# An FFN's up products: the side work as a pipeline of one step per product, sums of the weights ahead of their splits

## The chip, the cores and the metric

One core of a Trainium2 chip runs the whole kernel. The metric is device time in microseconds from the first to the last instruction, the median of several runs. In the profile PE is the engine for matrix products (its weight loads are listed apart as PEld), ACT, DVE and POOL are the engines for elementwise work (ScalarE, VectorE, GpSimd), and SP issues the transfers (DMAs). Each engine takes its own instructions strictly in order; an instruction that must wait holds up all that stand behind it on that engine.

## The reference

One block of a model with three mixers (a gated delta rule, an mLSTM and an S5 scan, with a projection before and one behind them), then the feed-forward part that matters here, for 2048 tokens, width 1024 and hidden width 2816, all in float32:

```python
def conv_ffn(x, w_up, conv_w, conv_b, w_down):
    h = causal_depthwise_conv(x @ w_up, conv_w) + conv_b      # 3 taps per channel
    gate, up = jnp.split(h, 2, axis=-1)
    return (jax.nn.silu(gate) * up) @ w_down
...
        x = x + y @ w_out[l]
        x = x + conv_ffn(rms_norm(x, norm2_w[l]), w_up[l], ffn_conv_w[l], ffn_conv_b[l], w_down[l])
    return rms_norm(x, final_norm_w)
```

## The kernel before, in words

**Stages.** The mixers and `out_proj` take about the first half of the span, then comes the feed-forward part: two halves of 1024 tokens, each with an up phase and a down phase. In an up phase `up_pair(hf, i)` is run for 22 pairs; pair i holds 128 gate columns and the 128 up columns that belong to them. After the 22 pairs the down phase multiplies two blocks of 512 tokens with `w_down`.

**Products.** The up product of a pair is a 2 x 2 block product (columns gate and up; tokens in two blocks of 512; the inner dimension of 1024 in two halves) done with 7 block products instead of 8. Each operand is split into a hi and a lo part of the matmul's type, and hi x hi, hi x lo and lo x hi are summed: 3 matmuls for each of 4 inner tiles, so 12 matmuls for a product and 84 for a pair. In the profile they are `psf<-bh,f_ph`, `psf<-bl,f_ph` and `psf<-bh,f_pl`; down products are called psd.

**Operands.** The token operands (`bh` from ACT, `bl` from DVE) are made once for each half, from the normed tokens in `h2_d`, by `build` (in a first version also by `first_build` while `out_proj` still runs, and by `rest_build` at the start of the first up phase). The weight operands are made anew for each pair. SP loads the two raw tiles `f_wr` of a pair (512 KB each, 4 buffers, so two pairs). POOL makes sums: S1 = a21 + a22, S2 = S1 - a11 (tiles `f_S`), a21 := a11 - a21 in place (`f_wr<-f_wr`), and S2' = a12 - S2. `split_part` makes a part out of a block: ACT copies it to the hi tile `f_ph`, POOL subtracts that from the block to give `f_pl`. The 7 parts of a pair are, in this order, of a11, S2, S1, a21, a22, a12, S2'. A ring holds 8 parts; `make()` makes one part each time it is called, once behind each product, and so part k of the next pair behind product k of this one.

**Behind a product.** `up_pair` takes what the 7 products give out of PSUM: `s1` is copied by ACT (`f_s`), DVE adds others to it (`f_u`, `f_w`), and from product 3 on the raw tiles of the result come (`f_rw`, DVE reading PSUM): r22 and r21 (up columns), r11 and r12 (gate columns). `conv` makes the 3 taps of a raw tile: ACT scales it with a bias into `f_cv` and copies two columns of halo in and out (`f_rw<-f_halo`, `f_halo<-f_rw`); DVE adds the two other taps (SCALAR_TENSOR_TENSOR, below also "taps"). `mid` lets ACT do silu on a gate tile, DVE multiply it by its up tile, and SP store it to `mid_d`, which the down phase reads.

**Order.** The order in the code of `up_pair` is the order in each engine's queue; other generators (operands, end of the layer before) are fitted in between by a planner, `drive`, by estimated times. In the kernel before, `conv` and `mid` run where they are called, each waiting for the one before, and `make()` runs after the work of its product.

## Time and profile before

| | |
|---|---|
| median of 3 runs | 3215.14 us (3211.07 to 3228.27) |
| profiled execution | 3215.11 us, span 3213.3 us |
| busy over the span | PE 87%, DVE 58%, ACT 41%, POOL 42% |
| first and last matmul of the first up phase | 1555.4 and about 2105 us |
| the second up phase | 2377 to 2932 us |
| granted PE clock, mean | 0.94 |

The profiled execution stands at the median. All engines' lines read "line engine operation out<-in", with the shapes, the count and the times; nearly all instructions carry the line of one helper, so the tile names tell what they are. Where a matmul's row ends in a bracket, it holds the idle time of PE before it and what ended it.

### The profile page before, as it was taken

How to read it: one execution, taken by the hardware profiler on the slowest of the kernel's cores; microseconds unless marked ns; L12 is line 12 of the kernel's file. 1: busy time of each engine (PE TensorE's matmuls, PEld its weight loads, DVE VectorE, ACT ScalarE, POOL GpSimd, SP SyncE). 2: the span in 40 equal slices, each digit the busy share in tenths (PEclk: the TensorE clock that was granted, in tenths of full speed). 3: DMA queues.
4: the chain of work that ended last, by engine and by line, in shares of the span. 5: the costliest groups of instructions: out<-in, count | busy, mean ns of one | idle time of the engine just before them, and what ended most of it. 6: DMA issues, size and time to landing. Idle time of an engine off the chain costs nothing. (4 is left out here: it accounts for less than half of the span.)

```text
span 3213.3 us, 39006 instructions
## 1 busy us (share of the span) xinstructions
PE 2804.3 (87%) x13298; PEld 2261.1 (70%) x13298; DVE 1862.8 (58%) x4296; ACT 1305.6 (41%) x2818; POOL 1342.9 (42%) x1046
## 2 busy tenths in 40 slices
PE   7796888979988897998888888889989888888997
PEld 5675777868877785877666666668767666666876
DVE  6874677687657866536455555573335555554143
ACT  4534354445443545224334433453223333344232
POOL 3350222223222422111455556545545555655553
PEclk9897899989999998999899999999989999998999
DMA  4222212232213333266322222154531222223443
GB/s 120 83 76 84 73 56 72 74 92 84 62 55 90 89 108 118 76 219 195 115 65 59 62 64 72 60 177 167 171 115 59 59 63 68 67 59 126 162 156 113
DMA packets 366540, 312.17 MB, mean 97 GB/s; under 512 B 41283, under 2 KB 303558, under 8 KB 366342
## 3 DMA queue, kind: packets, MB, share of 16 engines
q1 hardware_dynamic: 366342, 309.69, 31.3%
q8 instruction: 105, 1.72, 0.2%
q14 instruction: 93, 0.76, 0.1%
HBM read 244.48 MB, written 65.14 MB: 96 GB/s over the span
## 5 line engine op out<-in xcount | busy, mean ns | idle before, releaser
L169 POOL TENSOR_TENSOR f_pl<-f_wr,f_ph 128x512 fp32r<-128x512 f32 x360 | 520.6, 1462 | 576.3 <-ACT f_ph L169 576.3
L169 PE MATMUL psf<-bh,f_ph 128*128 128x512 f32 x1232 | 515.9, 419 | 93.6 <-ACT f_ph L169 85.3
L169 DVE SCALAR_TENSOR_TENSOR f_cv<-f_rw,fpar,f_cv 128x512 f32<-128x512 f32 x352 | 344.3, 989 | 399.7 <-ACT f_rw L169 393.4
L169 PE MATMUL psf<-bh,f_pl 128*128 128x512 f32 x1232 | 520.1, 422 | 50.0 <-POOL f_pl L169 49.3
L169 PE MATMUL psf<-bl,f_ph 128*128 128x512 f32 x1232 | 507.0, 411 | 0.6 <-DVE bl L169 0.6
L169 POOL TENSOR_TENSOR wl<-wr,wh 128x1024 fp32r<-128x1024 f32 x108 | 258.2, 2393 | 582.0 <-ACT wh L169 511.9
L169 PEld LDWEIGHTS psf<-bh,f_ph 128*128 128x128 f32 x1232 | 244.3, 198 | 177.3 <-ACT f_ph L169 116.7
L169 ACT ACTIVATE f_ph<-f_wr 128x512 fp32r<-128x512 f32 x360 | 216.7, 621 | 369.5 <-issue 179.5
L169 PEld LDWEIGHTS psf<-bh,f_pl 128*128 128x128 f32 x1232 | 244.2, 198 | 152.8 <-POOL f_pl L169 97.2
L169 PEld LDWEIGHTS psf<-bl,f_ph 128*128 128x128 f32 x1232 | 244.5, 198 | 58.1 <-DVE bl L169 1.1
L169 PE MATMUL psd<-f_ph,d_l 128*128 128x512 f32 x640 | 253.4, 396 | 18.2 <-DVE d_l L169 18.1
L169 PE MATMUL psd<-f_ph,d_h 128*128 128x512 f32 x640 | 252.5, 395 | 4.8 <-ACT d_h L169 4.8
L169 PE MATMUL psd<-f_pl,d_h 128*128 128x512 f32 x640 | 252.1, 394 | 0.1
L169 POOL TENSOR_TENSOR f_pl<-f_S,f_ph 128x512 fp32r<-128x512 f32 x132 | 169.0, 1294 | 143.2 <-ACT f_ph L169 138.0
L169 DVE TENSOR_TENSOR d_l<-d_x,d_h 128x512 fp32r<-128x512 f32 x80 | 69.5, 875 | 269.5 <-ACT d_h L169 260.9
L169 ACT ACTIVATE f_cv<-f_rw,fpar 128x512 f32<-128x512 f32 x176 | 142.4, 809 | 180.9 <-DVE f_rw L169 180.9
L169 ACT ACTIVATE f_ph<-f_S 128x512 fp32r<-128x512 f32 x132 | 77.8, 621 | 204.9 <-POOL f_S L169 204.9
L169 PEld LDWEIGHTS psd<-f_ph,d_l 128*128 128x128 f32 x640 | 121.9, 190 | 47.9 <-DVE d_l L169 22.7
L169 PEld LDWEIGHTS psd<-f_ph,d_h 128*128 128x128 f32 x640 | 122.2, 191 | 30.8 <-ACT d_h L169 5.6
L169 PEld LDWEIGHTS psd<-f_pl,d_h 128*128 128x128 f32 x640 | 122.1, 191 | 26.4 <-POOL f_pl L169 0.7
L169 ACT ACTIVATE wh<-wr 128x1024 fp32r<-128x1024 f32 x108 | 114.1, 1056 | 39.6 <-PE psz L169 17.9
L169 ACT ACT_TABLE_LOAD x83 | 106.5, 1283 | 32.2 <-DVE acc L169 29.5
(514 smaller groups left out, 6144.2 us busy)
## 6 DMA issues: line engine op xcount, KB each, us to landing
wr<-in_w_in_dram SPq DMA_DIRECT2D x104, 512.0 KB
f_wr<-in_w_up_dram SPq DMA_DIRECT2D x88, 512.0 KB
f_wr<-in_w_down_dram SPq DMA_DIRECT2D x88, 512.0 KB
mid_d<-f_cv SPq DMA_DIRECT2D x88, 256.0 KB
d_x<-mid_d SPq DMA_DIRECT2D x80, 256.0 KB
xt<-in_x_dram SPq DMA_DIRECT2D x16, 512.0 KB
y<-y_d SPq DMA_DIRECT2D x16, 512.0 KB
h_d<-n_h SPq DMA_DIRECT2D x32, 256.0 KB
```

Of the source, the lines that this page charges most:

```text
L169: return f(*args, **kw)
```

## The change

`up_pair` keeps a list, `self.later`, of work put off by a number of steps. Behind each product `due()` first runs what is due, then `make()`, and only then comes the product's own evacuation. `conv` is cut in two: ACT's share one step later, DVE's two taps two steps later; `mid` puts silu three steps behind its call and the product with its store four. The list is emptied behind the last pair of a half. In `make`, S1 and S2 of a pair are computed right behind part 6 of the pair before (`sum12`), a21 in step 1 and S2' in step 4, each two steps ahead of its split. Raw tiles that come free are loaded again when the next `make()` goes through (`freed`). In `build`, the hi copies of a group are issued together, then the lo parts, then the sums, with places between them where the planner may put other work.

```diff
@@ -1574,9 +1574,11 @@
     def operands(self, pool, n):
         return [[pool.tile([P, 4, BT], F32R, name=f"b{e}{o}") for e in "hl"] for o in range(n)]
 
-    def put(self, o, j, x, cols=slice(0, BT)):
+    def put_hi(self, o, j, x, cols=slice(0, BT)):
+        self.A.activation(out=self.bq[o][0][:, j, cols], in_=x, func=AF.Copy)
+
+    def put_lo(self, o, j, x, cols=slice(0, BT)):
         hi, lo = [t[:, j, cols] for t in self.bq[o]]
-        self.A.activation(out=hi, in_=x, func=AF.Copy)
         self.V.tensor_tensor(out=lo, in0=x, in1=f32(hi), op=ALU.subtract)
 
     def h_part(self, x, hf, j, kh, n, cols=slice(0, BT)):
@@ -1591,17 +1593,24 @@
             for c0 in range(0, BT, W):
                 cols = slice(c0, c0 + W)
                 b11, b12, b21, b22 = [self.h_part(tile(), hf, j, kh, n, cols) for kh in range(2) for n in range(2)]
-                yield b12, b22
-                self.put(0, j, b11, cols)
-                if len(self.bq) > 5:
-                    self.put(5, j, b21, cols)
-                    self.put(6, j, b22, cols)
+                first = [(0, b11)] + ([(5, b21), (6, b22)] if len(self.bq) > 5 else [])
+                yield b11, b12, b21, b22
+                for o, x in first:
+                    self.put_hi(o, j, x, cols)
+                yield self.bq[first[-1][0]][0][:, j, cols], 1.0
+                for o, x in first:
+                    self.put_lo(o, j, x, cols)
                 V.tensor_tensor(out=b22, in0=b22, in1=b12, op=ALU.subtract)
                 V.tensor_tensor(out=b12, in0=b12, in1=b11, op=ALU.subtract)
                 V.tensor_tensor(out=b11, in0=b22, in1=b11, op=ALU.add)
                 V.tensor_tensor(out=b21, in0=b21, in1=b11, op=ALU.subtract)
-                for o, x in ((3, b22), (2, b12), (1, b11), (4, b21)):
-                    self.put(o, j, x, cols)
+                yield b21, 2.0
+                then = ((3, b22), (2, b12), (1, b11), (4, b21))
+                for o, x in then:
+                    self.put_hi(o, j, x, cols)
+                yield self.bq[4][0][:, j, cols], 1.0
+                for o, x in then:
+                    self.put_lo(o, j, x, cols)
         self.built = True
 
     def first_build(self):
@@ -1613,7 +1622,8 @@
             for j in range(4):
                 x = self.h_part(tile(), 0, j, 1, n)
                 yield x
-                self.put(5 + n, j, x)
+                self.put_hi(5 + n, j, x)
+                self.put_lo(5 + n, j, x)
         self.rest = True
 
     def ffn_plan(self):
@@ -1629,6 +1639,7 @@
                 self.loads += [("M", hf * HALF + q * BT)] + [("D", m) for m in range(MF)]
         self.raws, self.parts, self.ring = [], [], NPART
         self.built = False
+        self.freed, self.sums, self.later = 0, None, []
         for _ in range(NRAW):
             self.raw_load()
 
@@ -1660,38 +1671,41 @@
         kind, j = self.todo[0]
         if kind == "U" and self.fu is None:
             return
+
+        while self.freed:
+            self.freed -= 1
+            self.raw_load()
         self.todo.pop(0)
         if kind != "U":
             w = self.raws.pop(0)
             for c in range(2):
                 self.split_part(w[:, 4 * c:4 * c + 4, :])
-            self.raw_load()
+            self.freed += 1
             return
         gate, up = self.raws[0:2]
         a11, a12, a21, a22 = gate[:, 0:4, :], gate[:, 4:8, :], up[:, 0:4, :], up[:, 4:8, :]
-        if j == 0:
-            self.split_part(a11)
-        elif j == 1:
-            self.s1, self.s2 = [self.fu.tile([P, 4, P], F32, tag="f_" + nm, bufs=2, name="f_" + nm)
-                                for nm in ("S1", "S2")]
-            G.tensor_tensor(out=self.s1, in0=a21, in1=a22, op=ALU.add)
-            G.tensor_tensor(out=self.s2, in0=self.s1, in1=a11, op=ALU.subtract)
-            self.split_part(self.s2)
-        elif j == 2:
-            self.split_part(self.s1)
-        elif j == 3:
+
+        if j == 0 and self.sums is None:
+            self.sum12()
+        if j == 1:
             G.tensor_tensor(out=a21, in0=a11, in1=a21, op=ALU.subtract)
-            self.split_part(a21)
         elif j == 4:
-            self.split_part(a22)
-        elif j == 5:
-            self.split_part(a12)
-        else:
-            G.tensor_tensor(out=self.s2, in0=a12, in1=self.s2, op=ALU.subtract)
-            self.split_part(self.s2)
+            G.tensor_tensor(out=self.sums[1], in0=a12, in1=self.sums[1], op=ALU.subtract)
+        s1, s2 = self.sums
+        self.split_part((a11, s2, s1, a21, a22, a12, s2)[j])
+        if j == 6:
             self.raws = self.raws[2:]
-            for _ in range(2):
-                self.raw_load()
+            self.freed += 2
+            self.sums = None
+            if self.todo and self.todo[0][0] == "U":
+                self.sum12()
+
+    def sum12(self):
+
+        gate, up = self.raws[0:2]
+        s1, s2 = self.sums = [self.fu.tile([P, 4, P], F32, tag="f_" + nm, bufs=2, name="f_" + nm) for nm in ("S1", "S2")]
+        self.G.tensor_tensor(out=s1, in0=up[:, 0:4, :], in1=up[:, 4:8, :], op=ALU.add)
+        self.G.tensor_tensor(out=s2, in0=s1, in1=gate[:, 0:4, :], op=ALU.subtract)
 
     def bank(self):
         tag = min(self.bufs, key=lambda n: self.clock.slot(n, self.bufs[n]))
@@ -1713,23 +1727,42 @@
             self.ring += 1
             return ps
 
+        def due():
+            now, self.later = [f for d, f in self.later if d == 0], [(d - 1, f) for d, f in self.later if d]
+            for f in now:
+                f()
+            self.make()
+
         def conv(rw, ci):
+
             halo = self.halo2[:, ci, :]
-            cv = tile("cv", 5)
-            A.activation(out=cv, in_=rw[:, 2:BT + 2], func=AF.Identity,
-                         scale=self.fpar[:, 2, ci:ci + 1], bias=self.fpar[:, 3, ci:ci + 1])
-            A.activation(out=rw[:, 0:2], in_=halo, func=AF.Copy)
-            A.activation(out=halo, in_=rw[:, BT:BT + 2], func=AF.Copy)
-            for j in range(2):
-                V.scalar_tensor_tensor(out=cv, in0=rw[:, j:j + BT], scalar=self.fpar[:, j, ci:ci + 1],
-                                       in1=cv, op0=ALU.mult, op1=ALU.add)
+            cv = []
+
+            def first():
+                cv.append(tile("cv", 5))
+                A.activation(out=cv[0], in_=rw[:, 2:BT + 2], func=AF.Identity,
+                             scale=self.fpar[:, 2, ci:ci + 1], bias=self.fpar[:, 3, ci:ci + 1])
+                A.activation(out=rw[:, 0:2], in_=halo, func=AF.Copy)
+                A.activation(out=halo, in_=rw[:, BT:BT + 2], func=AF.Copy)
+
+            def second():
+                for j in range(2):
+                    V.scalar_tensor_tensor(out=cv[0], in0=rw[:, j:j + BT], scalar=self.fpar[:, j, ci:ci + 1],
+                                           in1=cv[0], op0=ALU.mult, op1=ALU.add)
+
+            self.later += [(0, first), (1, second)]
             return cv
 
         def mid(ga, up, n):
-            A.activation(out=ga, in_=ga, func=AF.Silu)
-            V.tensor_tensor(out=ga, in0=ga, in1=up, op=ALU.mult)
-            t0 = hf * HALF + n * BT
-            S.dma_start(out=self.mid_d[i, :, t0:t0 + BT], in_=ga)
+            def first():
+                A.activation(out=ga[0], in_=ga[0], func=AF.Silu)
+
+            def second():
+                V.tensor_tensor(out=ga[0], in0=ga[0], in1=up[0], op=ALU.mult)
+                t0 = hf * HALF + n * BT
+                S.dma_start(out=self.mid_d[i, :, t0:t0 + BT], in_=ga[0])
+
+            self.later += [(2, first), (3, second)]
 
         def raw(ps, b):
             rw = tile("rw", 4, BT + 2)
@@ -1738,36 +1771,38 @@
 
         g, u = i, MF + i
         ps = yield from prod(0)
+        due()
         s1 = tile("s1", 2)
         A.activation(out=s1, in_=ps, func=AF.Copy)
-        self.make()
         ps = yield from prod(1)
+        due()
         u2 = tile("u2", 1)
         add(u2, ps, s1)
-        self.make()
         ps = yield from prod(2)
+        due()
         w5 = tile("w5", 1)
         add(w5, ps, u2)
-        self.make()
         ps = yield from prod(3)
+        due()
         u3 = tile("u3", 1)
         add(u3, ps, u2)
         r22 = raw(ps, w5)
-        self.make()
         ps = yield from prod(4)
         yield lambda: self.rest
+        due()
         r21 = raw(ps, u3)
         up1 = conv(r21, u)
         up2 = conv(r22, u)
-        self.make()
         ps = yield from prod(5)
-        ga1 = conv(raw(ps, s1), g)
+        due()
+        r11 = raw(ps, s1)
+        ga1 = conv(r11, g)
         mid(ga1, up1, 0)
-        self.make()
         ps = yield from prod(6)
-        ga2 = conv(raw(ps, w5), g)
+        due()
+        r12 = raw(ps, w5)
+        ga2 = conv(r12, g)
         mid(ga2, up2, 1)
-        self.make()
 
     def down(self, blk, dn):
 
@@ -1869,7 +1904,9 @@
                     yield lambda: self.built
                 for i in range(MF):
                     yield from self.up_pair(hf, i)
-                self.fu = None
+                for _, f in sorted(self.later, key=lambda x: x[0]):
+                    f()
+                self.later, self.fu = [], None
             with ExitStack() as c:
                 dn = self.pool("dn", side="right", ctx=c)
                 if hf + 1 < NH:
```

The first place in the queues is ACT in one steady pair of the first up phase (`f_ph` are the hi copies, `f_cv<-f_rw,fpar` the first tap, `f_cv<-f_cv` silu). Before, from `f_s` of one pair on:

```order
L169 ACTIVATE f_s_16948<-psf 128x512
L169 ACTIVATE f_ph<-f_wr 128x512
L169 ACTIVATE f_ph<-f_S_16970 128x512
L169 ACTIVATE f_ph<-f_S_16969 128x512
L169 ACTIVATE f_ph<-f_wr 128x512
L169 ACTIVATE f_cv<-f_rw,fpar 128x512
L169 ACTIVATE f_rw<-f_halo 128x2
L169 ACTIVATE f_halo<-f_rw 128x2
L169 ACTIVATE f_cv<-f_rw,fpar 128x512
```

and after, from the first tap of the last gate tile of the pair before on:

```order
L169 ACTIVATE f_cv<-f_rw,fpar 128x512
L169 ACTIVATE f_rw<-f_halo 128x2
L169 ACTIVATE f_halo<-f_rw 128x2
L169 ACTIVATE f_ph<-f_wr 128x512
L169 ACTIVATE f_s_16948<-psf 128x512
L169 ACTIVATE f_cv<-f_cv 128x512
L169 ACTIVATE f_ph<-f_S_16916 128x512
L169 ACTIVATE f_cv<-f_cv 128x512
L169 ACTIVATE f_ph<-f_S_16915 128x512
L169 ACTIVATE f_ph<-f_wr 128x512 x2
```

The last gate tile's first tap and both silus of a pair now stand among the first three steps of the next pair, and part 0's copy stands ahead of `f_s`.

The second place is DVE in one steady pair (`f_cv<-f_rw,fpar,f_cv` are taps, `f_cv<-f_cv` is the product with the up tile, the rows with psf read PSUM). Before:

```order
L169 TENSOR_TENSOR f_u_15392<-psf,f_s_15373 128x512
L169 TENSOR_TENSOR f_w_15415<-psf,f_u_15392 128x512
L169 TENSOR_TENSOR f_u_15434<-psf,f_u_15392 128x512
L169 TENSOR_TENSOR f_rw<-psf,f_w_15415 128x512
L169 TENSOR_TENSOR f_rw<-psf,f_u_15434 128x512
L169 SCALAR_TENSOR_TENSOR f_cv<-f_rw,fpar,f_cv 128x512 x4
L169 TENSOR_TENSOR f_rw<-psf,f_s_15373 128x512
L169 SCALAR_TENSOR_TENSOR f_cv<-f_rw,fpar,f_cv 128x512 x2
L169 TENSOR_TENSOR f_cv<-f_cv 128x512
L169 TENSOR_TENSOR f_rw<-psf,f_w_15415 128x512
L169 SCALAR_TENSOR_TENSOR f_cv<-f_rw,fpar,f_cv 128x512 x2
L169 TENSOR_TENSOR f_cv<-f_cv 128x512
```

and after, from the read of product 5 on:

```order
L169 TENSOR_TENSOR f_rw<-psf,f_s_15373 128x512
L169 SCALAR_TENSOR_TENSOR f_cv<-f_rw,fpar,f_cv 128x512 x4
L169 TENSOR_TENSOR f_rw<-psf,f_w_15418 128x512
L169 SCALAR_TENSOR_TENSOR f_cv<-f_rw,fpar,f_cv 128x512 x4
L169 TENSOR_TENSOR f_u_15571<-psf,f_s_15548 128x512
L169 TENSOR_TENSOR f_cv<-f_cv 128x512
L169 TENSOR_TENSOR f_w_15593<-psf,f_u_15571 128x512
L169 TENSOR_TENSOR f_cv<-f_cv 128x512
L169 TENSOR_TENSOR f_u_15614<-psf,f_u_15571 128x512
L169 TENSOR_TENSOR f_rw<-psf,f_w_15593 128x512
L169 TENSOR_TENSOR f_rw<-psf,f_u_15614 128x512
```

The gate tiles' four taps now stand behind the read of product 6, ahead of the next pair's first sum, and the two products with the up tile between the sums of the next pair.

The third place is POOL at the start of the second up phase (the row with x92 or x93 is the run of lo parts of the first down phase; the x93 holds part 0 of the next up phase too). Before:

```order
L169 TENSOR_TENSOR f_pl<-f_wr,f_ph 128x512 x93
L169 TENSOR_TENSOR f_S_19870<-f_wr 128x512
L169 TENSOR_TENSOR f_S_19871<-f_S_19870,f_wr 128x512
L169 TENSOR_TENSOR f_pl<-f_S_19871,f_ph 128x512
L169 TENSOR_TENSOR f_pl<-f_S_19870,f_ph 128x512
L169 TENSOR_TENSOR f_wr<-f_wr 128x512
```

and after:

```order
L169 TENSOR_TENSOR f_pl<-f_wr,f_ph 128x512 x92
L169 TENSOR_TENSOR f_S_19866<-f_wr 128x512
L169 TENSOR_TENSOR f_S_19867<-f_S_19866,f_wr 128x512
L169 TENSOR_TENSOR f_pl<-f_wr,f_ph 128x512
L169 TENSOR_TENSOR f_wr<-f_wr 128x512
L169 TENSOR_TENSOR f_pl<-f_S_19867,f_ph 128x512
```

Part 0's lo now stands behind both sums, and a21's sum stands ahead of S2's lo.

## The prediction

> **What bounds the kernel now.** I first cut the span into its stages with the table of windows: the two up phases, one stretch inside the first, and one in the down stage after it. Its columns are the window, its length, the busy time of PE with its instructions in brackets, then PEld, DVE, ACT and POOL, the granted clock, and the DMA share with GB/s.
>
> ```profile
> 1555.00:2105.00 550.00, 480.11 (x1852) 359.22 (x1851) 294.65 (x373) 219.51 (x484) 320.93 (x245) 0.95 0.23 68
> 2377.00:2932.00 555.00, 482.48 (x1848) 359.58 (x1849) 305.87 (x417) 214.45 (x478) 324.03 (x246) 0.94 0.22 66
> 1700.00:2000.00 300.00, 261.77 (x1009) 194.34 (x1008) 163.23 (x205) 118.61 (x265) 174.10 (x132) 0.95 0.22 64
> 2270.00:2370.00 100.00, 100.00 (x442) 82.77 (x441) 16.98 (x24) 28.98 (x54) 47.88 (x32) 1.00 0.49 166
> ```
>
> The up phases take 550 + 555 = 1105 us for 44 pairs of columns. In them no engine is full: of the 300 us in the middle PE is busy for 87%, DVE for 54%, ACT for 40%, POOL for 58%. In the down stage PE is full, at clock 1.00. So in the up phases something other than throughput sets the pace. PE's timeline there (start, duration, and in brackets the idle time before and who ended it) gives its pace and its gaps:
>
> ```profile
> 1759.29 0.39 PE L169 MATMUL psf<-bh,f_ph 128*128 128x512 f32 x1
> ...
> 1763.97 0.39 PE L169 MATMUL psf<-bh,f_pl 128*128 128x512 f32 x1
> ...
> 1772.85 0.50 PE L169 MATMUL psf<-bh,f_pl 128*128 128x512 f32 x1 [0.63 <-POOL f_pl L169]
> 1776.61 0.50 PE L169 MATMUL psf<-bh,f_ph 128*128 128x512 f32 x1 [1.15 <-ACT f_ph L169]
> ```
>
> From the first to the second of these rows there are 20 steps in 4.68 us: 0.234 us a matmul at full clock. A pair has 7 products of 12 matmuls, so PE alone needs 84 x 0.234 = 19.66 us. What a pair takes is seen from ACT, which copies product 0 of each pair into `s1`:
>
> ```profile
> 1751.55 0.57 ACT L169 ACTIVATE f_s<-psf 128x512 f32<-128x512 f32 x1
> ...
> 1776.46 0.58 ACT L169 ACTIVATE f_s<-psf 128x512 f32<-128x512 f32 x1
> ```
>
> That is 24.91 us, 5.25 over PE's own need. The rest is gaps in which PE waits for a weight part (`f_ph` from ACT, `f_pl` from POOL), and a lower clock behind them: the window that holds the last gap, and the next two, read
>
> ```profile
> 1776.00:1780.00 4.00, 2.77 (x7) 0.79 0.53 144
> 1780.00:1784.00 4.00, 4.00 (x15) 0.79 0.65 184
> 1784.00:1788.00 4.00, 4.00 (x18) 1.00 0.00 0
> ```
>
> so 8 us x 0.21 = 1.7 us is the clock's share after such a gap. Why are the parts late, with 7 of them made ahead? The table of waits over 1700 to 2000 (who waits for whom, us in total, times, longest) says:
>
> ```profile
> POOL f_pl L169 <- ACT f_ph L169: 121.2, 59, 4.9
> DVE f_cv L169 <- ACT f_rw L169: 112.5, 36, 7.5
> ACT f_ph L169 <- POOL f_S L169: 51.0, 12, 4.3
> ACT f_cv L169 <- DVE f_rw L169: 47.4, 24, 3.1
> ACT f_cv L169 <- DVE f_cv L169: 42.2, 25, 2.0
> ACT f_ph L169 <- POOL f_wr L169: 40.5, 12, 3.4
> ```
>
> ACT, DVE and POOL wait for each other in a ring, each in order: ACT stands 51.0 + 40.5 + 47.4 + 42.2 = 181.1 us of 300 (15.1 us a pair at 12 pairs) behind a sum on POOL or a step of the convolution on DVE; POOL's lo parts and DVE's two taps stand behind ACT. The side chain has a period of 24.9 us although it has at most 14.5 us of work for an engine. It is the bound, and PE idles for it.
>
> **The change, part by part.** The work does not change in number; it moves. What a pair costs each side engine comes from these rows (busy, mean ns):
>
> ```profile
> L169 POOL TENSOR_TENSOR f_pl<-f_wr,f_ph 128x512 fp32r<-128x512 f32 x77 | 109.8, 1426 | 132.5 <-ACT f_ph L169 132.5
> L169 POOL TENSOR_TENSOR f_S<-f_wr 128x512 f32<-128x512 f32 x20 | 25.9, 1294 | 0.0
> L169 ACT ACTIVATE f_cv<-f_rw,fpar 128x512 f32<-128x512 f32 x76 | 61.4, 809 | 75.1 <-DVE f_rw L169 75.1
> L169 ACT ACTIVATE f_ph<-f_wr 128x512 fp32r<-128x512 f32 x77 | 47.8, 621 | 64.2 <-POOL f_wr L169 64.2
> L169 ACT ACTIVATE f_cv<-f_cv 128x512 f32<-128x512 f32 x39 | 24.6, 630 | 65.7 <-DVE f_cv L169 65.7
> L169 ACT ACTIVATE f_halo<-f_rw 128x2 f32<-128x2 f32 x76 | 15.5, 204 | 2.4
> L169 DVE TENSOR_TENSOR f_cv<-f_cv 128x512 f32<-128x512 f32 x39 | 27.0, 692 | 27.2 <-ACT f_cv L169 27.2
> L169 DVE SCALAR_TENSOR_TENSOR f_cv<-f_rw,fpar,f_cv x352: 743/752/1782, 1588.8 to 2944.2; 128x512 f32<-128x512 f32 x176
> ...
> 1753.56 0.68 DVE L169 TENSOR_TENSOR f_u<-psf,f_u 128x512 f32<-128x512 f32 x1
> 1754.16 0.68 DVE L169 TENSOR_TENSOR f_rw<-psf,f_w 128x512 f32<-128x512 f32 x1
> ```
>
> (1) *Sums ahead of splits, hi one step ahead of who needs it.* S1 and S2 now run after part 6 of the pair before, a21 in step 1 for step 3, S2' in step 4 for step 6. The two ACT waits on POOL go: 91.5 us in 12 pairs, 7.6 us a pair. (2) *Convolution in two steps, silu and product in two more.* ACT's share of a convolution runs in the step after its raw tile, DVE's two taps one step later, silu after that, the product last. ACT's other 89.6 us (7.5 a pair) and DVE's wait for `f_rw` go likewise. What is late next? ACT by itself has 7 x 0.62 + 4 x (0.81 and two halo copies of about 0.2) + 2 silus at 0.63 and the `s1` copy at 0.57, 11.0 us: far below 19.66. POOL has 11 operations at 1.29, 14.2 us. DVE has 8 taps at 0.752, 2 products at 0.692 and 7 reads of PSUM, 0.60 apart when one follows the other: 6.0 + 1.4 + 4.2 = 11.6 us. None is over 19.66 alone. But POOL and DVE stretch each other, which the old waits have largely kept apart. At the end of the first up phase both have a queue:
>
> ```profile
> 2102.83 7.63 POOL L169 TENSOR_TENSOR f_pl<-f_wr,f_ph 128x512 fp32r<-128x512 f32 x5
> ...
> 2105.04 5.98 DVE L169 SCALAR_TENSOR_TENSOR f_cv<-f_rw,fpar,f_cv 128x512 f32<-128x512 f32 x4 [0.97 <-ACT f_rw L169]
> ```
>
> Five POOL operations alone would take about 5 x 1.25 = 6.25, three of them met taps: (7.63 - 6.25)/3 = 0.46 more for each. Four taps would take 3.0; they took 5.98, of which three or so met POOL: about 0.97 more each. If x of DVE's ten operations in a pair meet one of POOL's, POOL needs 14.2 + 0.46x and DVE 11.6 + 0.97x. x = 10 gives POOL 18.8 and DVE 21.3; x = 7.7, which is what is left for meeting when POOL also runs through the 4.2 us of DVE's PSUM reads (3.3 of its 11), gives DVE 19.1. So a pair lies between PE's 19.66 and 21.3. In the new order DVE has only one read each in steps 4 and 5, while POOL has three operations there, so I take the lower end with a remainder of 0.23 a pair, 10 us in all; the whole span of this term is 0 to 44 x 1.64 = 72 us.
>
> The Trainium skill, page "SBUF — State Buffer", section "SBUF: two separate sides", speaks against the change here: VectorE operations with two SBUF inputs and GpSimd operations take one shared port pair as an exclusive lock for the whole instruction. By it a pair would need 14.2 + 8 x 0.752 + 2 x 0.692 = 21.6 us of that port and the sum below would be 44 x 1.94 - 10 = 75 us higher, 3080. The row above agrees that they hinder each other, but not for the whole of the instruction: a POOL operation and a tap together took 1.71, not 2.04.
>
> (3) *Loads of raw weights one step later.* They were issued in part 6's step, now in the next step, and S1 needs them six products, 16.8 us, later. What two loads take:
>
> ```profile
> 1753.40:1758.50 5.10, 5.10 (x23) 1.00 0.82 214
> 1759.30:1764.30 5.00, 5.00 (x23) 1.00 0.00 0
> ```
>
> 1 MB within about 5 us. Hidden, with 11 us to spare; between them SP issues only the two stores of `mid` of a pair. Cost 0; if this cover went, POOL would stand at S1 and all lo parts behind it.
>
> (4) *Starts of the phases.* These stay or grow:
>
> ```profile
> 1580.05 0.80 PE L169 MATMUL psf<-bh,f_ph 128*128 128x512 f32 x1 [8.33 <-ACT bh L169]
> ...
> 2390.00 1.26 POOL L169 TENSOR_TENSOR f_S<-f_S,f_wr 128x512 f32<-128x512 f32 x1 [10.23 <-DVE d_ss L169]
> ...
> 2391.97 0.80 PE L169 MATMUL psf<-bh,f_ph 128*128 128x512 f32 x1 [9.24 <-ACT f_ph L169]
> ```
>
> The first is `rest_build`'s operands: 8.3 us plus 2 for the clock behind it, kept. In the second phase S2 waits until 2390 for memory that the down stage's last rows still use; now S1 and S2 stand ahead of part 0's lo on POOL, so product 0 stops as well: 9.2 + 3 + 2. In out_proj the last build unit (five copies by ACT) stands ahead of part 0: +3, between 0 and +6.
>
> (5) *Ends of the phases.* PE's first down products wait for the last evacuations:
>
> ```profile
> 2116.18 0.80 PE L169 MATMUL psd<-f_ph 128*128 128x512 f32 x1 [3.53 <-DVE f_rw L169]
> ...
> 2938.03 0.76 PE L169 MATMUL psd<-f_ph 128*128 128x512 f32 x1 [5.16 <-DVE f_rw L169]
> 2942.44 0.80 PE L169 MATMUL psd<-f_ph 128*128 128x512 f32 x1 [2.80 <-DVE f_rw L169]
> ```
>
> 11.5 us. The last two raw tiles no longer stand behind silu and product, only behind four taps (3 to 6 us): I take -8, between 0 and -11.5. The `build` of the next half is only reordered inside the down stage, which has ACT and DVE mostly free (29 and 17 us of 100): 0, +-3.
>
> **Sum**, against the profiled execution of 3215.11 us, which is the median's 3215.14: up phases 44 x 19.66 = 865, plus 10 remainder, plus starts 10.3 + 14.2, about 25, together 900 instead of 1105: -205; ends -8; out_proj +3. 3215 - 210 = 3005.
>
> **Rivals.** (a) *DVE with POOL becomes the bound.* Taps meet POOL nearly always, a pair takes 20.6 to 21.3: 41 to 72 us instead of the remainder of 10, so 3036 to 3067. For it: both are busier per us than before, and DVE's six port operations of steps 6 and 0 come while POOL has five. Against it: the free steps 4 and 5. (b) *The clock.* If PE, now with fewer gaps, still has 0.95 granted on average, a pair takes 19.66/0.95 = 20.7 and 44 x 1.03 = 45 us stand in place of the remainder of 10: 3040. Against it is the 1.00 of the down window. (c) *Nothing gained.* If a wait I do not see keeps the ring closed (a tile that comes free late), pairs stay at 24.9 and the time at 3200 to 3230. (d) *Slower: the load that is late.* S1 blocks POOL in order until the two raws have landed, so a landing of L us from step 0 delays everything by L - 16.8 in each pair; with the 5 us slack PE has left, it turns slower where L is above 22, at 44 us per us beyond: 24 would be 3300. The trace has 5.
>
> **How the numbers follow.** A main case (PE-bound with small gaps, 2978 to 3035) has 0.73, (a) 0.17, (b) 0.04, (c) 0.03, (d) 0.02, a still better case below 2978 0.01. The low end is the sum without remainder (-10), with `rest_build`'s stall hidden (-10) and ends and out_proj at their best (-7); the high end takes in (a) up to its dearest and 6 for starts that I mis-sized: 2978 to 3073. Half a per cent, 16 us, is what a measurement can tell from no change: faster 0.95, same 0.03, slower 0.02.
>
> **What would show it.** Right: `f_s` 19.7 to 20 us apart; the windows of the up phases at clock 0.99 or 1.00 and PE over 97% busy; ACT's waits on `f_S`, `f_wr` and `f_cv` near zero; the tap's mean above 989 ns and POOL's f_pl above 1426, since they meet more; up phases of about 448 and 452 us. Rival (a) shows as PE waiting for f_pl or for banks read by DVE, with DVE over 95% busy. Wrong would be a pair that stays at 24 us, or PE gaps whose releaser is a DMA of f_wr.

## The result, and the profile after

The changed kernel takes 2995.05 us (median of 4 runs, 2987.35 to 2996.64) against 3217.19 us of the kernel before: a ratio of 0.930, with a 95% interval of 0.927 to 0.933. The prediction was 3005. The profiled execution took 2995.83 us with a span of 2994.1. By stages of the two profiled executions:

| stage | before, us | after, us | change |
|---|---|---|---|
| up to the first matmul of out_proj | 1296.0 | 1304.9 | +8.9 |
| out_proj, up to the first psf | 259.4 | 271.7 | +12.3 |
| first up phase | 550.0 | 440.5 | -109.5 |
| first down phase | 271.8 | 256.4 | -15.4 |
| second up phase | 554.8 | 448.7 | -106.1 |
| second down phase, to the last matmul | 262.1 | 252.7 | -9.4 |
| tail | 19.2 | 19.2 | 0 |

The first row's code is the same in both. Over the kernels below, which all share it, it came out between 1296.8 and 1309.9, so its 8.9 us say nothing of the change.

The table of windows for the up phases of the changed kernel, with a stretch inside the first (same columns as before):

```profile
1576.60:2017.10 440.50, 436.83 (x1849) 349.55 (x1850) 382.58 (x379) 219.17 (x494) 383.55 (x247) 0.99 0.28 88
2273.50:2722.30 448.80, 435.78 (x1849) 349.93 (x1850) 388.80 (x419) 213.83 (x486) 386.31 (x248) 0.98 0.27 86
1700.00:1950.00 250.00, 250.00 (x1069) 200.99 (x1068) 223.19 (x217) 122.57 (x280) 219.69 (x140) 1.00 0.26 81
```

PE is busy for the whole of the 250 us, at a granted clock of 1.00. The copies of product 0 by ACT stand 19.68 us apart:

```profile
1787.00 0.58 ACT L169 ACTIVATE f_s<-psf 128x512 f32<-128x512 f32 x1
...
1806.68 0.58 ACT L169 ACTIVATE f_s<-psf 128x512 f32<-128x512 f32 x1
```

That is the time of PE's own 84 matmuls (19.66) and nothing else. The whole table of waits over 1700 to 1950 now has four rows:

```profile
ACT f_cv L169 <- DVE f_rw L169: 97.1, 25, 4.7
POOL f_pl L169 <- ACT f_ph L169: 28.5, 27, 1.2
ACT f_cv L169 <- DVE f_cv L169: 27.7, 13, 2.1
DVE f_rw L169 <- PE psf L169: 27.0, 13, 2.1
```

No row has PE waiting. ACT's waits on POOL's sums are gone. Its waits on DVE are still there (97.1 + 27.7 us in 13 pairs, against 47.4 + 42.2 in 12 before), but they hold up nothing that PE needs. The last row is new and tells most: DVE waits for PE once in each pair, 2.1 us. The side has become the one that waits.

### The profile page after: what moved, and what is told of

It reads as the page before. It is cut to its first block, busy times and chain, and to the rows that moved or that the text cites. A ratio compares the mean times of both kernels' runs of the same rounds, so it can differ in the third digit from the quotient of the medians.

```text
span 2994.1 us, 38977 instructions
## 1 busy us (share of the span) xinstructions
PE 2715.9 (91%) x13298; PEld 2245.8 (75%) x13298; DVE 2042.5 (68%) x4296; ACT 1299.6 (43%) x2818; POOL 1461.7 (49%) x1046
## 4 chain that ended last, share of the span: by engine, by line
PE 50%; DVE 6%; ACT 1%; DMA 1%; POOL 1%; issue 1%; SPq 0%; DVEq 0%; ACTq 0%; POOLq 0%
PE psf L169 28%; PE psd L169 14%; PE pso L169 5%; DVE d_ss L169 1%; DVE d_rs L169 1%; DVE d_a L169 1%; DVE bl L169 1%; POOL f_pl L169 0%; DVE acc L169 0%; DMA d_x<-mid_d 0%; DVE f_cv L169 0%; DMA y<-y_d 0%; PE sd_pw L169 0%; PE pz L169 0%; PE psx L169 0%
## 5 line engine op out<-in xcount | busy, mean ns | idle before, releaser
L169 POOL TENSOR_TENSOR f_pl<-f_wr,f_ph 128x512 fp32r<-128x512 f32 x360 | 541.2, 1518 | 337.2 <-ACT f_ph L169 320.3
L169 PE MATMUL psf<-bh,f_pl 128*128 128x512 f32 x1232 | 490.6, 398 | 13.3 <-POOL f_pl L169 13.3
L169 PE MATMUL psf<-bh,f_ph 128*128 128x512 f32 x1232 | 490.6, 398 | 5.5 <-ACT f_ph L169 5.0
L169 PE MATMUL psf<-bl,f_ph 128*128 128x512 f32 x1232 | 490.5, 398 | 2.8 <-DVE bl L169 2.8
L169 DVE SCALAR_TENSOR_TENSOR f_cv<-f_rw,fpar,f_cv 128x512 f32<-128x512 f32 x352 | 479.2, 1381 | 6.7 <-ACT f_rw L169 0.4
L169 PEld LDWEIGHTS psf<-bh,f_pl 128*128 128x128 f32 x1232 | 233.2, 189 | 71.2 <-POOL f_pl L169 14.5
L169 PEld LDWEIGHTS psf<-bh,f_ph 128*128 128x128 f32 x1232 | 233.3, 189 | 63.5 <-ACT f_ph L169 5.8
L169 PEld LDWEIGHTS psf<-bl,f_ph 128*128 128x128 f32 x1232 | 233.2, 189 | 60.8 <-DVE bl L169 4.0
L169 PE MATMUL psd<-f_ph,d_l 128*128 128x512 f32 x640 | 252.3, 394 | 17.1 <-DVE d_l L169 17.1
L169 POOL TENSOR_TENSOR f_pl<-f_S,f_ph 128x512 fp32r<-128x512 f32 x132 | 220.8, 1674 | 4.5 <-ACT f_ph L169 0.2
L169 PEld LDWEIGHTS psd<-f_pl,d_h 128*128 128x128 f32 x640 | 121.4, 190 | 25.5
L169 POOL TENSOR_TENSOR yl<-y,yh 128x1024 fp32r<-128x1024 f32 x16 | 39.2, 2451 | 177.7 <-ACT yh L169 177.7
```

The lines of the kernel that those rows point to most:

```text
L169: return f(*args, **kw)
```

## Experiments

All times are medians, the ratios are against the kernel before on the same chip. Differences of a few us between variants are read with their intervals.

**One half of the change at a time.** Both halves keep the new `build`. First the convolution pipeline with `make()` as before:

```diff
-        if j == 0 and self.sums is None:
-            self.sum12()
-        if j == 1:
-            G.tensor_tensor(out=a21, in0=a11, in1=a21, op=ALU.subtract)
...
+        elif j == 1:
+            self.s1, self.s2 = [self.fu.tile([P, 4, P], F32, tag="f_" + nm, bufs=2, name="f_" + nm)
+                                for nm in ("S1", "S2")]
+            G.tensor_tensor(out=self.s1, in0=a21, in1=a22, op=ALU.add)
+            G.tensor_tensor(out=self.s2, in0=self.s1, in1=a11, op=ALU.subtract)
+            self.split_part(self.s2)
...
+            for _ in range(2):
+                self.raw_load()
```

> The changed kernel with make() as before: sums stand in the step of their own split and ACT waits for them there (7.6 us a pair before), raw loads go at once; the convolution pipeline stays. Theory 'the waits of the ring add up': 24.9 less the 7.5 us of ACT's waits on the convolution is 17.4, below PE's 19.66, so this part alone gives nearly all: 2995 to 3015 us, pairs at 19.7. Theory 'POOL's own chain': POOL has 14.2 us of work, four waits of 0.74 for a hi copy that itself waits for a sum, and 8 x 0.46 of stretching by the taps, 20.9 us, so pairs at 20 to 21.5 and 3010 to 3080 us. Theory 'both parts are needed': one ring of waits is enough to hold the period, pairs above 23 us, over 3130 us.

Measured: 3032.48 us, ratio 0.942 (0.941 to 0.944). Pairs are 20.24 us apart (`f_s` at 1703.50, 1723.73, 1743.97). The waits of 1700 to 2000:

```profile
ACT f_ph L169 <- POOL f_S L169: 88.0, 30, 3.8
POOL f_pl L169 <- ACT f_ph L169: 58.3, 72, 1.2
ACT f_ph L169 <- POOL f_wr L169: 49.9, 15, 3.3
DVE f_cv L169 <- ACT f_rw L169: 30.5, 15, 2.0
```

ACT behind POOL's sums, and POOL behind ACT's copies: this is the second case that was expected, POOL's own chain with its handovers (20 to 21.5 us; its estimate was 20.9). So the pipeline of the convolution alone brings 4.7 of the 5.2 us a pair. Then the other half, the sums ahead of their splits with `up_pair` as before:

```diff
         ps = yield from prod(5)
-        due()
-        r11 = raw(ps, s1)
-        ga1 = conv(r11, g)
+        ga1 = conv(raw(ps, s1), g)
         mid(ga1, up1, 0)
+        self.make()
```

> The changed kernel with up_pair as before: convolution, silu and product are issued at once behind their raw tile, and make() after them; only the sums stand ahead of their splits (and the loads one step later). Theory 'the waits add up': 24.9 - 7.6 = 17.3 us, so PE-bound, 2995 to 3015 us. Theory 'the chain ACT-DVE of products 4 to 6 holds': r21, taps, r11, first tap, taps, silu, product, r12, first tap, taps, silu is about 16 us plus ACT's five copies of 2.7 us and PE's own products in between, 20 to 22 us a pair, 3010 to 3100 us. Theory 'both parts are needed': above 23 us a pair, over 3130.

Measured: 3158.05 us, ratio 0.981 (0.980 to 0.982), pairs 23.43 us apart. That is the third case, in which both parts are needed (above 23 us a pair, over 3130); the adding up of waits and the chain from ACT to DVE, at 20 to 22 us, both missed it. The rows of 1700 to 2000:

```profile
POOL f_pl L169 <- ACT f_ph L169: 106.1, 26, 4.9
ACT f_cv L169 <- DVE f_rw L169: 82.8, 26, 5.5
DVE f_cv L169 <- ACT f_rw L169: 75.3, 38, 4.2
...
ACT f_ph L169 <- POOL f_S L169: 39.1, 13, 3.0
```

ACT's wait for DVE's `f_rw` grew from 47.4 to 82.8 us, while its waits for sums fell only from 51.0 and 40.5 to 39.1 and 17.3 (the last of these rows is not shown): waits moved more than they went. One half alone brings 4.7, the other 1.5, together 6.2; both in one kernel bring 5.2. PE's 19.66 would cut the gain off there; what the side chain itself does is seen only with a lighter PE.

**The side chain's own pace.** In the product loop two of the three matmuls are kept, in the changed kernel and in the one before:

```diff
-            yield from self.mm3(ps, [(hi[:, k, :], lo[:, k, :], bh[:, k, :], bl[:, k, :]) for k in range(4)])
+            for k in range(4):
+                self.T.matmul(out=ps, lhsT=hi[:, k, :], rhs=bh[:, k, :], start=k == 0, stop=False)
+                self.T.matmul(out=ps, lhsT=lo[:, k, :], rhs=bh[:, k, :], start=False, stop=k == 3)
+                yield ()
```

> The kernel before with two of three matmuls in the up products. Theory 'the ring of waits sets 24.9 us and PE only idles': pairs stay at 24.9 us within 0.3, the total within 15 us of the kernel before. Rival 'PE is a link of the ring' (ACT's copy of product 0 and DVE's reads wait for it): pairs fall by up to a third of the 19.66 us, to 20 to 23 us, total 3050 to 3150.

Measured: 3225.23 us in one run. The pairs of the kernel before stay where they were, with a third of the matmuls taken away:

```profile
1714.90 0.58 ACT L169 ACTIVATE f_s<-psf 128x512 f32<-128x512 f32 x1
...
1739.71 0.58 ACT L169 ACTIVATE f_s<-psf 128x512 f32<-128x512 f32 x1
```

24.81 us. In time the cut is less than a third: PE is busy for 17.6 us of a pair instead of 21.7, at a granted clock of 0.84 where it was 0.95. But the pair does not follow even that, so PE was no link of the chain that set the pace. And the same with the change:

> The changed kernel with two of three matmuls in the up products (hi x lo is left out), so PE needs 56 x 0.234 = 13.1 us a pair and the side work is the same. It shows the side chain's own period. If POOL needs 14.2 + 0.46x and DVE 11.6 + 0.97x with x near 6.5 as the changed kernel's tap mean of 1.415 us gives, pairs take 17.5 to 19.1 us (total about 2910 to 2965 us). If the shared port were held for whole instructions, 21.6 us. If the sides have much room, 13.1 to 16 us.

Measured: 2948.23 us in one run, with pairs 18.55 us apart:

```profile
1704.46 0.58 ACT L169 ACTIVATE f_s<-psf 128x512 f32<-128x512 f32 x1
...
1741.56 0.58 ACT L169 ACTIVATE f_s<-psf 128x512 f32<-128x512 f32 x1
```

(Two pairs lie between these rows.) So the change took the side chain from 24.8 to 18.55 us, 6.3 off, which the two halves' 6.2 agree with. PE needs 19.66: 1.1 us of room. The window's row shows what bounds the side now, DVE with 233.2 and POOL with 224.7 of 240 us (the third and fifth busy times):

```profile
1700.00:1940.00 240.00, 198.13 (x718) 143.41 (x719) 233.22 (x222) 124.14 (x283) 224.65 (x144) 0.91 0.27 85
```

How thin that room is was measured with two more POOL operations in each pair, S1 computed three times:

```diff
+        self.G.tensor_tensor(out=s1, in0=up[:, 0:4, :], in1=up[:, 4:8, :], op=ALU.add)
+        self.G.tensor_tensor(out=s1, in0=up[:, 0:4, :], in1=up[:, 4:8, :], op=ALU.add)
         self.G.tensor_tensor(out=s1, in0=up[:, 0:4, :], in1=up[:, 4:8, :], op=ALU.add)
```

> The changed kernel with S1 computed three times over, two more POOL operations in each pair and nothing else. With 8 of 12 matmuls the side chain took 18.55 us a pair, DVE busy for 97% and POOL for 94% of it. If that is the chain's own pace and POOL's operations add to it, two more at 1.3 to 1.74 us make it 21.1 to 22.0 us a pair, over PE's 19.66, and the total 60 to 105 us longer, 3055 to 3100 us. Rival 'there is room, POOL still waits 2.3 us a pair': 19.7 to 20.3 us, 2995 to 3020.

Measured: 3041.62 us in one run, pairs alternately 19.5 and 22.0 us long, 20.8 in the mean, POOL busy for 237.4 of 240 us. This lies between the two forecasts and nearer the first: POOL is full now, though the added operations were partly absorbed by its old 2.3 us of waiting.

**Loads at once.** The raw loads go out in the step that frees their tiles:

```diff
-            self.freed += 1
+            self.raw_load()
...
-            self.freed += 2
+            for _ in range(2):
+                self.raw_load()
```

> The changed kernel with the raw loads issued in the step that frees their tiles, as before the change. The prediction put the later issue at 0 since two loads land in 5 us and have 16.8. So the same within 4 us. Rival: SP's order matters at the phase ends (down weights, store of mid), 5 to 10 us in either direction.

Measured: 2991.54 us, ratio 0.930 (0.928 to 0.931): the same as the changed kernel's 0.930 (0.927 to 0.933). The later issue costs nothing that shows.

**out_proj's 12.3 us.** The old `build`, `first_build` and `rest_build` in the changed kernel:

```diff
-                yield self.bq[first[-1][0]][0][:, j, cols], 1.0
-                for o, x in first:
-                    self.put_lo(o, j, x, cols)
...
+                self.put(0, j, b11, cols)
...
+                for o, x in ((3, b22), (2, b12), (1, b11), (4, b21)):
+                    self.put(o, j, x, cols)
```

> The changed kernel with build, first_build and rest_build as before. In the profiled executions out_proj took 12.3 us longer after the change (259.4 to 271.7), which the prediction had at +3. Theory 'the cut build with its due times costs it, its last unit standing at the end of out_proj': out_proj falls by 9 to 14 us, the total to about 2983. Rival 'out_proj moved for another reason (the state it starts in)': the same within 4 us, 2995. Rival 'the cut build pays in the first pairs or in the down stage': out_proj gains but rest_build's stall of 8 us comes back, total 2990 to 3000.

Measured: 2980.74 us, ratio 0.926 (0.925 to 0.927), 14 us better than the change as made; the two intervals only touch, and out_proj gives most of it: it takes 259.2 us again (first pso at 1304.6, first psf at 1563.8). The timelines of DVE, ACT and SP at out_proj's last row tell why. PE's last pso product ends at 1559.6 in the changed kernel and at 1556.8 with the old build. In the changed kernel

```profile
1564.11 0.68 DVE L169 TENSOR_TENSOR o_x<-o_x,pso 128x512 f32<-128x512 f32 x1
```

```profile
1570.51 1.15 ACT L169 ACTIVATE o_x<-o_x,n_rs 128x1024 f32<-128x1024 f32 x1 [4.90 <-DMA x_d<-o_x]
```

```profile
1564.68 1.91 SPq L169 DMA_DIRECT2D n_b<-h_d  x4
1566.68 0.38 SPq L169 DMA_DIRECT2D x_d<-o_x  x1
```

and with the old build

```profile
1556.87 0.69 DVE L169 TENSOR_TENSOR o_x<-o_x,pso 128x512 f32<-128x512 f32 x1 [3.28 <-PE pso L169]
```

```profile
1560.96 1.15 ACT L169 ACTIVATE o_x<-o_x,n_rs 128x1024 f32<-128x1024 f32 x1 [2.59 <-DVE n_rs L169]
```

```profile
1557.59 0.33 SPq L169 DMA_DIRECT2D x_d<-o_x  x1
```

DVE adds the last product to the row, SP stores it, ACT scales it in place once the store is done, PE transposes it (psx), and then the first part comes. From the end of the last pso product to the first psf product this takes 17.1 us, with the old build 7.0, as in the kernel before. The 10.1 us between have three parts. DVE's addition ends 5.2 us after the product instead of 0.7, since it stands behind the row before and a build unit: 4.5 us. The scaling starts 5.7 us after the addition instead of 3.4; the unit's four loads stand ahead of the store on SP: 2.3 us. And from the transposes to the first psf product it takes 4.9 us instead of 1.6, since the unit's five copies stand ahead of part 0 on ACT and wait for DVE: 3.3 us. The rest of the 12.3, about 2 us, lies earlier in out_proj.

Which piece of the new build does this was asked in two steps. The pauses without their due times:

```diff
-                yield self.bq[first[-1][0]][0][:, j, cols], 1.0
+                yield self.bq[first[-1][0]][0][:, j, cols]
...
-                yield b21, 2.0
+                yield b21
...
-                yield self.bq[4][0][:, j, cols], 1.0
+                yield self.bq[4][0][:, j, cols]
```

> The changed kernel; in build the three pauses stay, but without their due times (1.0 and 2.0 us). With the old build out_proj went from 271.7 to 259.2 us, and the trace of the changed kernel shows the last row's store x_d<-o_x on SP behind the four loads of the last build unit, and ACT's scaling of that row waiting 4.9 us for that store. Theory 'the due times make each unit slip by a row, so that the last one stands between the last row's steps': without them the units come earlier, 2981 to 2986 us. Rival 'the pauses themselves, or all hi copies ahead of the lo parts': no change, 2995.

Measured: 2990.11 us, ratio 0.929 (0.927 to 0.931), which is not apart from the change; in its profile out_proj still took 275.5 us. The due times are not it. Then no pauses at all, with the hi copies still first:

```diff
-                yield self.bq[first[-1][0]][0][:, j, cols], 1.0
...
-                yield b21, 2.0
...
-                yield self.bq[4][0][:, j, cols], 1.0
```

> The changed kernel with build in one piece again, all hi copies of a group ahead of its lo parts as in the change, but without the three pauses inside. The order then has no build unit between the last rows of out_proj. Theory 'the pauses let units slip behind later rows': 2978 to 2985 us, as with the old build (2980.7). Rival 'hi copies first is what costs': 2990 to 2996.

Measured: 2980.48 us, ratio 0.926 (0.924 to 0.927), out_proj 256.4 us, and the same 7.0 us behind the last pso product as with the old build. The pauses are the cause. With them the last unit stands between the last row's own steps, as the rows above show; that the planner fits rows of out_proj into each pause until it comes to that is how I read them.

**The start of the second up phase.** In the changed kernel PE waits there for 13.0 us, because POOL's S2 waits for memory that the last rows of the down phase still use:

```profile
2284.27 1.26 POOL L169 TENSOR_TENSOR f_S<-f_S,f_wr 128x512 f32<-128x512 f32 x1 [28.58 <-DVE d_ss L169]
...
2287.25 0.80 PE L169 MATMUL psf<-bh,f_pl 128*128 128x512 f32 x1 [13.01 <-POOL f_pl L169]
```

Three ways round it were tried. Part 0 ahead of the sums:

```diff
         if j == 0 and self.sums is None:
+            self.split_part(a11)
             self.sum12()
+            return
```

> The changed kernel, but at the start of a phase part 0 is split ahead of the sums S1 and S2. Theory: product 0 of the second up phase then does not wait for the memory that S2 needs; PE's wait there falls from 13.0 to about 10 us, and 3 us are gained in all (2992). Rival: the end of that wait is fixed and PE waits as long behind product 0 in any case, 0 us.

Measured: 2998.62 us, ratio 0.932 (0.930 to 0.933): no gain. Product 0 goes through and PE waits behind it instead, 11.5 us in all:

```profile
2274.89 0.80 PE L169 MATMUL psf<-bh,f_pl 128*128 128x512 f32 x1 [0.61 <-POOL f_pl L169]
2288.31 0.80 PE L169 MATMUL psf<-bh,f_ph 128*128 128x512 f32 x1 [9.36 <-ACT f_ph L169]
2291.01 0.80 PE L169 MATMUL psf<-bh,f_pl 128*128 128x512 f32 x1 [1.48 <-POOL f_pl L169]
```

Then other memory for the sums (with the old build, so these two compare with 2980.74):

```diff
-        s1, s2 = self.sums = [self.fu.tile([P, 4, P], F32, tag="f_" + nm, bufs=2, name="f_" + nm) for nm in ("S1", "S2")]
+        s1, s2 = self.sums = [self.fu.tile([P, 4, P], F32, tag="f_S", bufs=4, name="f_" + nm) for nm in ("S1", "S2")]
```

> The changed kernel with the old build, and S1 and S2 from one rotating set of four tiles, so that the first S2 of a phase lies where the down phase's input tiles were, which come free early, and not where its last output rows are. Theory: POOL's wait of 28.6 us and PE's of 13.0 at the start of the second up phase go, 10 us less than with the old build alone: about 2971 us. Rival: another tile of the phase's first steps lies on the output rows now and PE waits as long for that: 2981.

Measured: 2984.66 us, ratio 0.927 (0.925 to 0.928). My guess of where the output rows lie was wrong; the wait moved and grew to 16.2 us:

```profile
2275.76 1.26 POOL L169 TENSOR_TENSOR f_S<-f_S,f_wr 128x512 f32<-128x512 f32 x1 [32.22 <-DMA out_dram<-d_a]
```

And the other way, with tiles of the later steps set aside ahead of them:

```diff
                 self.fu = self.pool("fu", side="right", ctx=c)
+                for nm, n, wd in (("cv", 5, BT), ("rw", 4, BT + 2), ("s1", 2, BT)):
+                    self.fu.tile([P, wd], F32, tag="f_" + nm, bufs=n, name="f_" + nm)
```

> The changed kernel with the old build, and the tiles of convolution and product 0 set aside ahead of the sums in the phase's memory, so that S1 and S2 lie higher, off the region in which the wait was longer when they were moved down. Theory: the wait of PE at the start of the second up phase (13.0 us) goes, 2970 us. Rival: the whole region is held by the last output rows until then, or the first convolution tiles wait instead: 2978 to 2986.

Measured: 2979.69 us, ratio 0.926 (0.924 to 0.927). The 13.0 us are gone (0.96 is left), but nothing is gained, since other waits come in the next pair:

```profile
2274.32 0.60 ACT L169 ACTIVATE f_s<-psf 128x512 f32<-128x512 f32 x1 [8.38 <-DVE d_ss L169]
```

```profile
2285.63 1.26 POOL L169 TENSOR_TENSOR f_S<-f_wr 128x512 f32<-128x512 f32 x1 [17.14 <-DMA f_wr<-in_w_up_dram]
```

Now ACT's copy of product 0 waits for DVE's work on the output rows, so its tile seems to lie there, and POOL reaches the second pair's S1 before its raw tile has landed, so PE waits 8.3 us there. The three versions near 2980 us (old build, no pauses, this one) cannot be told apart; each is about 14 us better than the change as made.

## Why the prediction was right, and which terms were off

**The bound, and parts 1 and 2.** Right. The side chain held 24.9 us also with less for PE to do (24.81 with a third of the matmuls left out), and with the change the pair is PE's 19.66. The remainder of 10 us for gaps was not needed: no gap is left in 250 us. What was wrong is the way I put waits to parts: 7.6 us a pair for the sums and 7.5 for the convolution would have given a side chain near 10 us if they came off in full. It fell by 6.3, to 18.55. One of the signs that I named is wrong for the same reason: ACT's waits on `f_cv` were to be near zero, and they are 9.8 us a pair where they were 7.5. They cost nothing, since no row has PE waiting, but they did not go. Waits in a ring of engines that work in order replace each other, and a table of them bounds no gain; what bounded it was the busy time of DVE and POOL with its stretching.

**The stretching of POOL and DVE.** It was sized somewhat too high, and it is the reason why there is only 1.1 us of room. Groups of the changed kernel over 1600 to 1980:

```profile
L169 DVE SCALAR_TENSOR_TENSOR f_cv<-f_rw,fpar,f_cv 128x512 f32<-128x512 f32 x156 | 217.7, 1415 | 3.2 <-ACT f_rw L169 0.4
L169 DVE TENSOR_TENSOR f_cv<-f_cv 128x512 f32<-128x512 f32 x38 | 45.0, 1184 | 0.0
L169 POOL TENSOR_TENSOR f_S<-f_wr 128x512 f32<-128x512 f32 x20 | 34.8, 1738 | 0.0
L169 POOL TENSOR_TENSOR f_S<-f_wr,f_S 128x512 f32<-128x512 f32 x19 | 24.7, 1298 | 0.0
L169 DVE TENSOR_TENSOR f_rw<-psf,f_w 128x512 f32<-128x512 f32 x38 | 25.7, 677 | 0.0
```

A tap went from a mean of 985 ns in the same window of the kernel before to 1415, the product with the up tile from 692 to 1184. Over their undisturbed times that is 8 x 0.66 + 2 x 0.49 = 6.3 us a pair; at 0.97 for each meeting x is 6.5, under the 7.7 that I had taken as the least. (Its own rows give 0.99, (5.98 - 3.0) / 3.) Two of POOL's sums show where they meet: S1, in step 6 with the taps, takes 1.74 us; S2', in step 4 where DVE only reads PSUM, 1.30. DVE's reads of PSUM stayed at 0.68. How they meet is seen in single rows:

```profile
1768.73 1.75 POOL L169 TENSOR_TENSOR f_wr<-f_wr 128x512 f32<-128x512 f32 x1
1769.36 1.67 DVE L169 SCALAR_TENSOR_TENSOR f_cv<-f_rw,fpar,f_cv 128x512 f32<-128x512 f32 x1
...
1773.26 1.18 DVE L169 TENSOR_TENSOR f_cv<-f_cv 128x512 f32<-128x512 f32 x1
1773.85 1.75 POOL L169 TENSOR_TENSOR f_pl<-f_wr,f_ph 128x512 fp32r<-128x512 f32 x1
```

The tap ends at 1771.03, 0.55 us after the POOL operation that began before it (1770.48); the second POOL operation ends at 1775.60, 1.16 after the product that began before it (1774.44). It is so at every meeting between 1640 and 1980 us, 0.55 to 0.56 and 1.14 to 1.17. They take turns, and a turn of each together is 1.70 us where the two alone take 0.75 + 1.29 = 2.04. By the Trainium skill's page "SBUF — State Buffer", section "SBUF: two separate sides", whichever of the two starts first gets the shared port pair for the whole instruction and the other fully blocks. The turns agree with that; the 21.6 us a pair that the prediction worked out from it, with whole durations, is refuted by 19.68 and by 18.55, since some 0.3 us of each pair of turns overlap. An estimate with the turns in place of the durations, 11 x 1.15 for POOL and 10 x 0.55 for DVE's taps and products, is 18.2 us a pair: near the 18.55 with the lighter PE, and with two more POOL operations 20.5, near the 20.8 of S1 three times. So what bounds the side chain now seems to be the turns of the two together; no run here tests this apart from the two sums. The other half of what that page of the Trainium skill states, that it is DVE operations with two SBUF inputs that contend with GpSimd's, agrees with the rows: those that read one operand from PSUM are not stretched.

**Part 3, the loads.** Right: 0 (2991.54 with them issued at once). The rival built on it, a sum that waits for its raw tile, does exist at one place: at the start of the second up phase, once the wait ahead of it is gone (17.1 us).

**Part 4, the starts.** The second phase was right (9.2 + 3 forecast, 13.0 measured). So was the sum of the starts: over 22 x 19.66 us the up phases took 8.0 and 16.2, where 10.3 and 14.2 were forecast. But the first came near by luck, since its stall was mis-sized, and so was out_proj. `rest_build`'s stall did not stay: of 8.3 us there are left

```profile
1595.23 0.49 PE L169 MATMUL psf<-bh,f_ph 128*128 128x512 f32 x1 [0.54 <-ACT bh L169]
1597.07 0.50 PE L169 MATMUL psf<-bl,f_ph 128*128 128x512 f32 x1 [1.34 <-DVE bl L169]
1598.76 0.50 PE L169 MATMUL psf<-bl,f_ph 128*128 128x512 f32 x1 [0.73 <-DVE bl L169]
1600.45 0.50 PE L169 MATMUL psf<-bl,f_ph 128*128 128x512 f32 x1 [0.73 <-DVE bl L169]
```

3.3 us, with the clock undisturbed (1.00 from 1590 to 1602); most of the rest of the 8.0 comes with a granted clock of 0.88 over the phase's first 28 us. With the old build the stall is small too (0.81 and 1.74), so the new `rest_build` is not what took it away. The two half changes, which both have it, tell what did. With the convolution's pipeline alone, ACT still behind POOL's sums, the stall is there:

```profile
1605.65 0.79 PE L169 MATMUL psf<-bh,f_ph 128*128 128x512 f32 x1 [8.69 <-ACT bh L169]
```

With the sums ahead of their splits alone it is gone:

```profile
1595.49 0.49 PE L169 MATMUL psf<-bh,f_ph 128*128 128x512 f32 x1 [0.83 <-ACT bh L169]
```

So the stall goes with the place of the sums: ACT comes to those copies 25.5 us after the phase's first product in the former, behind waits of 4.2 and 3.3 us for a sum, and 18.0 us after it in the latter. And out_proj was forecast at +3, in 0 to +6, and took +12.3: I had counted ACT's five copies, which cost the 3.3 us above, and put at nothing DVE's addition behind the row before and a unit (4.5 us) and the unit's loads on SP ahead of the store that the last row waits for (2.3 us).

**Part 5, the ends.** Forecast -8, no more than -11.5; the down phases are 24.8 us shorter, and 20 to 26 us in the seven other kernels above that leave both halves and the work of PE and POOL as they are. Here the term was too small, and its range too. The table of windows for the first 40 us of the first down phase, before and after (PE alone):

```profile
2105.40:2145.40 40.00, 29.92 (x108) 0.86 0.60 205
```

```profile
2017.10:2057.10 40.00, 39.52 (x173) 1.00 0.63 213
```

65 matmuls more in the same time, nearly all of the 15.4 us. I had summed three gaps and left out two things: the lower clock among them, 0.86 over these 40 us, and this wait for the first input of the down products in the kernel before, of which 0.48 us is left:

```profile
2128.20 0.79 PE L169 MATMUL psd<-f_ph,d_h 128*128 128x512 f32 x1 [4.02 <-ACT d_h L169]
```

**The sum.** Up phases -215.6 where -205 was forecast, ends -25 for -8, out_proj +12.3 for +3, and +8.9 in code that is the same: -219, where -210 was forecast. Misses of both signs cancelled, so that 2995 for 3005 is in part luck: the mechanism was right, and the total is better than its terms.

## What to carry to other kernels

When no engine is full and each waits for the others in turn, leave out a third of PE's matmuls: if the period stays, the ring is the bound, and its new bound is what the side engines need with their stretching, not the old period less the waits removed. With a full step of slack behind each step, waits may stay where they are and cost nothing. A generator's pause is a place where others are put between: count what then stands ahead of the last row on each engine and on SP, and at the end of a stage leave no pause.

## What the runs showed of the hardware

A POOL operation of 1.29 us and a DVE operation with two SBUF inputs (a tap of 0.75) take turns where they meet: the DVE operation ends 0.55 us after POOL's and the POOL operation 1.15 us after DVE's. POOL operations that meet taps thus take 1.5 to 1.8 us and most of the taps 1.67 or 1.82, while DVE operations that read one operand from PSUM keep 0.68. Work of 14.2 us on POOL and 11.6 on DVE became 17 to 18 us on each, which makes them 88 and 89% busy in the changed kernel (219.7 and 223.2 of 250 us). The granted clock stayed at 1.00 through 250 us without a gap in PE, where it had been 0.95 with a gap every few products.
